# A two-layer decoder trunk: the first layer's down projection with tokens on partitions, turned back by transposes

## The chip, the cores and the metric

The kernel runs on one core of a Trainium2 chip. Times are device microseconds (us) of the whole execution. The kernel before took 593.86 us in the median of 3 runs (593.1 to 595.12).

## The reference

The input x has 256 tokens of 1024 features, in float32. Two layers follow each other. Layer 0 mixes tokens by DSA: an indexer scores all earlier tokens for each query, the 64 best are kept, and 8 heads attend over one shared latent. Layer 1 mixes by NSA: 8 heads attend over compressed blocks of keys and over two sets of keys and values (selected blocks and a window), and a gate weighs the three results. The keys and values of layer 1 are made once, from the stream behind layer 0. Each layer ends in the same MLP, and the output is normed. What the change touches is this:

```
def rmsnorm(x, g):
    y = x * rsqrt(mean(x * x, -1) + EPS)
    return y * g
x = x + relu(rmsnorm(x, g_mlp[l]) @ w_up[l]) ** 2 @ w_down[l]   # 1024 -> 4096 -> 1024
...
proj = rmsnorm(x, g_attn[0]) @ a_w_in[0]                        # head of layer 0
...
kv = rmsnorm(x, g_kv_shared) @ w_kv_shared                      # behind layer 0
```

## The kernel before, in words

Almost every operand of a product is split into a rounded part and a remainder, both in a format (fp32r) that TensorE takes in one pass. A product is then three matmuls (high by high, high by low, low by high), which `mm3` (line 96) issues. Weights come by DMA from SyncE's queue into 5 raw buffers; `weights` and `colw` (lines 135 to 149) let ScalarE round them (line 141) and VectorE form the remainder (line 142) into 8 weight buffers.

The stream is kept with features on partitions, as 8 tiles of 128 features by 256 tokens. The MLP (lines 776 to 819 for layer 0, from 1200 for layer 1) runs over 32 blocks of 128 hidden features. For block fi, `up` makes u (24 matmuls of 256 columns); ScalarE, GpSimd and VectorE square and split it; and the down projection of the block before adds to four PSUM banks. The last NDEF = 4 blocks are left for the end. In layer 0 the down projection is `KOuter` (line 597): the weight block is stationary, u's 256 tokens move, and the sum has features on partitions, so 24 matmuls of 256 columns per block. `finish` closes one bank after the other, each with an epilogue `end0` (line 812): VectorE adds the bank to the scaled stream x1 and gets x2 (512 columns); then for each of its two feature tiles ScalarE and VectorE form sh and sl (x2 times the gain, split) and ScalarE squares x2 for the norm; GpSimd adds the squares. In layer 1 the down projection has u stationary and 512 features of the weight block moving, so tokens are on partitions and a block takes 12 matmuls of 512 columns.

Behind layer 0 come the shared keys (line 830): kk, 96 matmuls that run over k = 0 to 7, the feature tiles of sh and sl, then kc (the tokens to be compressed, 4 times 24 matmuls by `projT`, in two banks), then the compressing products co, and the shared values v. The norm's factor is applied late: the mean of squares goes through a small matmul (after k = 4), VectorE and a power on GpSimd to r2; `bcast` (line 194, after k = 6) spreads r2 over all partitions by a matmul and a VectorE copy to Rb. Rb scales kk (line 863), kc (line 879) and the stream for layer 1 (xns on GpSimd, line 853).

At the head (lines 206 to 284) the input and a_w_in come in four pieces by SyncE's queue: the constants `vec` first, then xT and win of piece 0, 1, 2, 3. ScalarE's queue loads the bias table and its one-hot map. TensorE runs warm-up matmuls on ones, then the bias table's product `ups`, then the projection: 8 plain fp32 matmuls of 456 columns for piece 0 and 12 fp32r ones for each other piece. ScalarE squares xT (sqs), VectorE sums the squares and copies the projection out of its two banks (zc, line 314). One GpSimd power (line 355) gives three norm factors per token half, which the indexer's keys kd (line 362) and others wait for.

PSUM has 8 banks in two pools: psA (`acc=True`, 4 banks) and psB (4 banks). The framework orders instructions by its own estimate of time and adds all waits; `pin` keeps an instruction behind the one written before it on the same engine, and `behind(a, b)` issues a after b.

Of the kernel before, what the change touches and what calls it, by code (L numbers as in the profile page):

```python
# [50 lines left out]
def trunk(ctx: ExitStack, tc: tile.TileContext, I, out):  # L51
# [23 lines left out]
    def bigt(shape, dt, name):  # L75
        return big.tile(shape, dt, tag="big", name=name)
# [16 lines left out]
    def mm(ps, a, b, start, stop):  # L93
        return nc.tensor.matmul(ps, a, b, start=start, stop=stop, skip_group_check=True)  # L94

    def mm3(ps, ah, al, bh, bl, start, stop):
        mm(ps, ah, bh, start, False)
        mm(ps, ah, bl, False, False)
        mm(ps, al, bh, False, stop)

# [92 lines left out]

    def bcast(col2, name):

        ps = bank(name + "_ps")
        for i in range(2):
            mm(ps[:, i * P:(i + 1) * P], col2[:, i:i + 1].to_broadcast([P, P]), ident,
               i == 0, i == 1)
        b = kept([P, T], name)  # L200
        nc.vector.tensor_copy(b, ps[:, :T])
        return b


    new_phase("workA")
    vec = const.tile([P, NV], F32, name="vec")
    nc.sync.dma_start(vec, I["vecs"])
    mhalf = const.tile([P, 4], F32, name="mhalf")
# [15 lines left out]
    mm(ups[:H, :256], relb, oneh, True, True)  # L224
    for n in range(2):
        mm(wps[:, :P], ones, ones, True, True)
    usb = wk("pe", 4, [H, 384], "usb")
# [13 lines left out]

    xT = bigt([P, KT, T], F32, "xT")
    xgh = bigt([P, KT, T], F32R, "xgh")
# [6 lines left out]
    for j in range(4):  # L250
        pair = slice(2 * j, 2 * j + 2)
        nc.sync.dma_start(xT[:, pair], I["xT"][:, pair])
        raw = rawp.tile([P, 2, 456], F32, tag="raw", name=f"win{j}_raw")
        nc.sync.dma_start(raw.rearrange("p a m -> p (a m)"), I["a_w_in"][j])
        if j == 0:
            xg0 = k4([P, 2, T], "xg0")
            for k in range(2):
                nc.scalar.activation(xg0[:, k], xT[:, k], AF.Copy, scale=vec[:, V_GA + k:V_GA + k + 1])
        else:
            xh = nc.scalar.copy(xgh[:, pair], xT[:, pair])  # L260
            nc.vector.tensor_sub(xgl[:, pair], xT[:, pair], f(xgh[:, pair]))
            w = wp.tile([P, 2, 1024], F32R, tag="w", name=f"win{j}")
            wh, wl = (w[:, s, :912].rearrange("p (a m) -> p a m", a=2) for s in range(2))
            for a in range(2):
                g = vec[:, V_GA + 2 * j + a:V_GA + 2 * j + a + 1]
                hi_last = nc.scalar.activation(wh[:, a], raw[:, a], AF.Copy, scale=g)
                lo_last = nc.vector.scalar_tensor_tensor(wl[:, a], raw[:, a], g, f(wh[:, a]),
                                                         op0=OP.mult, op1=OP.subtract)
        for i in range(2):
            for a in range(2):  # L270
                k = 2 * j + a
                if j == 0:
                    mm(proj[i][:, :456], xg0[:, k, i * P:(i + 1) * P], raw[:, a], k == 0, False)
                    continue
                mm3(proj[i][:, :456], xgh[:, k, i * P:(i + 1) * P], xgl[:, k, i * P:(i + 1) * P],
                    wh[:, a], wl[:, a], False, k == KT - 1)
    for j in range(4):
        behind(nc.scalar.activation(sqs[:, j], xT[:, 2 * j:2 * j + 2], AF.Square), hi_last if j > 1 else xh)
    for j in range(1, 4):
# [74 lines left out]
    scs = const.tile([P, 2, 4], F32, name="scs")  # L354
    nc.gpsimd.tensor_tensor(scs[:, :, :3], ss[:, :, :3], mhalf[:, None, :3].to_broadcast([P, 2, 3]), op=OP.pow)
    pin(nc.gpsimd.tensor_tensor(scs[:, :, 3], msx, mhalf[:, :2], op=OP.pow))
# [420 lines left out]
    up = mlp_up(0, hh, hl, up_last)  # L777
    us, dws = {}, {}
    for fi in range(NF):
        us[fi] = up(fi)  # L780
        dws[fi] = colw(I["w_down"][0, fi], f"dn0_{fi}", after=up_last if fi < 2 else last if fi < 4 else None)
        if fi == 0:
            y = KOuter("y0")
        if 1 <= fi <= NF - NDEF:
            y.add(dws[fi - 1], us[fi - 1][:, 0], us[fi - 1][:, 1])
        if 4 <= fi < 4 + KT:
# [31 lines left out]

    y.finish([(dws[g], us[g][:, 0], us[g][:, 1]) for g in range(NF - NDEF, NF)], end0)


    new_phase("workN")
    def projT(ps, w, xh, xl, start):

        for k in range(KT):
            mm3(ps, w[0][:, k], w[1][:, k], xh[:, k], xl[:, k], start and k == 0, k == KT - 1)

# [5 lines left out]
    for k in range(KT):  # L833
        for g in range(G):
            for seg in range(2):
                wh, wl = kw[2 * g + seg]
                mm3(kk[g][:, seg * T:(seg + 1) * T], wh[:, k], wl[:, k], sh[:, k], sl[:, k],
                    k == 0 and seg == 0, k == KT - 1)
        if k == 4:
            ms2 = small([P, 2], "ms2")  # L840
# [4 lines left out]
            r2 = rsq(ms2, 2, "r2")  # L845
        if k == 6:
            Rb = bcast(r2, "Rb")

# [23 lines left out]
    for kv in range(2):  # L872
        ps = bank(f"kc{kv}")
        for g in range(G):
            projT(ps[:, g * T:(g + 1) * T], cw[2 * kv + g], sh, sl, g == 0)

# [510 lines left out]
```

## Time and profile before

| | |
|---|---|
| median of 3 runs | 593.86 us |
| the profiled execution | 593.29 us |
| its span (first to last instruction) | 591.5 us |
| TensorE busy with matmuls | 577.2 us, 98% |
| VectorE, ScalarE, GpSimd busy | 364.2, 320.4, 159.1 us |
| DMA | 103.97 MB, 176 GB/s mean |

The profiled execution lasted 1.79 us longer than its span. Matmuls overlap one another, so the duration of a single matmul is longer than the distance between the starts of two; the chain of waits, which follows the work that ended last, shows that distance in sums.

### The profile page before, as it was taken

How to read it: one execution, taken by the hardware profiler on the slowest of the kernel's cores; microseconds unless marked ns; L12 is line 12 of the kernel's file. 1: busy time of each engine (PE TensorE's matmuls, PEld its weight loads, DVE VectorE, ACT ScalarE, POOL GpSimd, SP SyncE). 2: the span in 40 equal slices, each digit the busy share in tenths (PEclk: the TensorE clock that was granted, in tenths of full speed). 3: DMA queues.
4: the chain of work that ended last, by engine and by line, in shares of the span. 5: the costliest groups of instructions: out<-in, count | busy, mean ns of one | idle time of the engine just before them, and what ended most of it. 6: DMA issues, size and time to landing. Idle time of an engine off the chain costs nothing.

```text
span 591.5 us, 10852 instructions
## 1 busy us (share of the span) xinstructions
PE 577.2 (98%) x4170; PEld 542.9 (92%) x4170; DVE 364.2 (62%) x612; ACT 320.4 (54%) x580; POOL 159.1 (27%) x225
## 2 busy tenths in 40 slices
PE   8899999999999999999999999999999999999995
PEld 6787899999999999999968999999899999999994
DVE  3897399544474444547897877639845444454523
ACT  6656666444444454436866878637544545454423
POOL 0155457010101011015530076808310110011012
PEclk9999999999999999999999999999999999999998
DMA  8911447765546656543499943314866665656201
GB/s 300 345 47 61 149 176 235 249 194 178 179 145 212 181 178 190 180 164 113 160 308 304 327 139 102 97 49 138 287 205 186 181 191 169 180 180 203 77 0 71
DMA packets 30475, 103.97 MB, mean 176 GB/s; under 512 B 3632, under 2 KB 5464, under 8 KB 30296
## 3 DMA queue, kind: packets, MB, share of 16 engines
q1 hardware_dynamic: 30024, 102.45, 53.7%
q10 hardware_dynamic: 400, 0.83, 0.5%
q8 instruction: 32, 0.52, 0.4%
q14 instruction: 19, 0.16, 0.1%
HBM read 102.21 MB, written 1.06 MB: 175 GB/s over the span
## 4 chain that ended last, share of the span: by engine, by line
PE 84%; DVE 9%; issue 2%; DMA 2%; ACT 1%; POOL 1%; SPq 1%; POOLq 0%; ACTq 0%; DVEq 0%
PE y L94 30%; PE u L94 28%; PE nq L94 4%; PE yb L94 3%; PE ya L94 3%; PE kk L94 2%; PE npo L94 2%; PE kc L94 1%; PE nl L94 1%; DVE c L903 1%; DMA win_raw<-in_a_w_in 1%; PE v L94 1%; PE co L94 1%; PE ix L94 1%; DMA wv_raw<-in_kvV 1%
## 5 line engine op out<-in xcount | busy, mean ns | idle before, releaser
L142 DVE TENSOR_TENSOR dn<-dn_raw,dn 128x1024 fp32r<-128x1024 f32 x64 | 80.6, 1260 | 99.2 <-ACT dn L141 99.2
L645 POOL TENSOR_TENSOR us<-ur 128x256 f32<-128x256 f32 x64 | 45.4, 711 | 282.0 <-ACT ur L642 282.0
L142 DVE TENSOR_TENSOR up<-up_raw,up 128x1024 fp32r<-128x1024 f32 x64 | 81.9, 1280 | 44.6 <-ACT up L141 44.6
L141 ACT CAST up<-up_raw 128x1024 fp32r<-128x1024 f32 x64 | 67.0, 1048 | 60.0 <-PE y L94 58.5
L94 PE MATMUL u<-h1h,up 128*128 128x256 f32 x512 | 97.0, 284 | 0.6 <-DVE up L142 0.6
L94 PE MATMUL y<-uu,dn 128*128 128x256 f32 x768 | 97.0, 283 | 0.3 <-DVE uu L647 0.3
L94 PE MATMUL u<-h0h,up 128*128 128x256 f32 x512 | 96.7, 283 | 0.0
L94 PEld LDWEIGHTS y<-uu,dn 128*128 128x128 f32 x768 | 94.2, 192 | 0.5 <-DVE uu L647 0.5
L94 PE MATMUL y<-dn,uu 128*128 128x512 f32 (+1 forms) x396 | 92.5, 384 | 0.0
L94 PEld LDWEIGHTS y<-dn,uu 128*128 128x128 f32 x396 | 71.1, 189 | 13.0
L94 PEld LDWEIGHTS u<-h1h,up 128*128 128x128 f32 x512 | 81.5, 191 | 1.6 <-DVE up L142 0.8
L642 ACT ACTIVATE ur<-u 128x256 f32<-128x256 f32 x64 | 24.6, 384 | 107.2 <-PE u L94 107.2
L94 PEld LDWEIGHTS u<-h0h,up 128*128 128x128 f32 x512 | 81.7, 192 | 0.0
L94 PE MATMUL u<-h1l,up 128*128 128x256 f32 x256 | 72.5, 283 | 0.0
L94 PE MATMUL u<-h0l,up 128*128 128x256 f32 x256 | 72.2, 283 | 0.0
L141 ACT CAST dn<-dn_raw 128x1024 fp32r<-128x1024 f32 x64 | 66.7, 1042 | 7.2 <-PE y L94 3.0
L94 PEld LDWEIGHTS u<-h1l,up 128*128 128x128 f32 x256 | 49.0, 191 | 0.9
L94 PEld LDWEIGHTS u<-h0l,up 128*128 128x128 f32 x256 | 49.1, 192 | 0.0
L647 DVE TENSOR_TENSOR uu<-us,uu 128x256 fp32r<-128x256 f32 x64 | 29.1, 455 | 8.1 <-POOL us L645 8.1
L646 ACT ACTIVATE uu<-ur 128x256 fp32r<-128x256 f32 x64 | 26.7, 417 | 0.1
L94 PE MATMUL ya<-oT,wo 128*128 128x256 f32 x192 | 25.2, 288 | 0.3 <-DVE oT L591 0.3
L94 PE MATMUL nq<-ah,wq 128*128 128x256 f32 x128 | 24.9, 286 | 0.0
(300 smaller groups left out, 966.8 us busy)
## 6 DMA issues: line engine op xcount, KB each, us to landing
up_raw<-in_w_up SPq DMA_DIRECT2D x64, 512.0 KB, 3.7
dn_raw<-in_w_down SPq DMA_DIRECT2D x64, 512.0 KB, 3.7
c1raw<-in_cmp_w SPq DMA_DIRECT2D x16, 512.0 KB, 4.9
wo_raw<-in_a_w_o SPq DMA_DIRECT2D x8, 512.0 KB, 4.1
wq_raw<-in_b_w_q SPq DMA_DIRECT2D x8, 512.0 KB, 5.9
wn_raw<-in_b_w_o SPq DMA_DIRECT2D x8, 512.0 KB, 4.9
wk_raw<-in_kvT SPq DMA_DIRECT2D x4, 512.0 KB, 3.6
wc_raw<-in_kvT SPq DMA_DIRECT2D x4, 512.0 KB, 3.6
```

The costliest lines, as they stand in the source:

```text
L94: return nc.tensor.matmul(ps, a, b, start=start, stop=stop, skip_group_check=True)
L141: ins = [hi(w[:, 0, :C], raw[:, :C]) if hi else nc.scalar.copy(w[:, 0, :C], raw[:, :C]), (lo or nc.vector).tensor_sub(w[:, 1, :C], raw[:, ...
L142: (lo or nc.vector).tensor_sub(w[:, 1, :C], raw[:, :C], f(w[:, 0, :C]))]
L642: nc.scalar.activation(r, ps[:, :T], AF.Relu)
L645: nc.gpsimd.tensor_tensor(s, r, r, op=OP.mult)
L646: nc.scalar.activation(u[:, 0], r, AF.Square)
L647: nc.vector.tensor_sub(u[:, 1], s, f(u[:, 0]))
L903: lo = nc.vector.tensor_sub(w4[:, :, 1], r4, f(w4[:, :, 0]))
```

## The change

It has four parts. The down projection of layer 0 takes layer 1's form (u stationary, 512 features moving, tokens on partitions). Its four banks yt[i][c] (token half i, feature half c) are closed in a written order, copied to SBUF by ScalarE (the last one half by VectorE), and 16 transposes by TensorE bring them back to features on partitions, from where `end0` goes on as before. The norm's small matmul moves behind k = 7, and `bcast` behind the first 24 matmuls of kc, whose banks now come from psA. At the head xT of piece 0 is issued first on SyncE's queue, and win of piece 0 and `vec` on ScalarE's; one warm-up matmul is added behind `ups` and three are pinned there; the squares of pieces 0 and 1 go behind the last split of the weights. The power of line 355 is cut in two: the keys' factor first.

```diff
-    def bcast(col2, name):
+    def bcast(col2, name, after):
...
-            mm(ps[:, i * P:(i + 1) * P], col2[:, i:i + 1].to_broadcast([P, P]), ident,
-               i == 0, i == 1)
+            behind(mm(ps[:, i * P:(i + 1) * P], col2[:, i:i + 1].to_broadcast([P, P]), ident, i == 0, i == 1), after)
...
+    xT = bigt([P, KT, T], F32, "xT")
+    pin(nc.sync.dma_start(xT[:, 0:2], I["xT"][:, 0:2]))
+    raw0 = rawp.tile([P, 2, 456], F32, tag="raw", name="win0_raw")
+    pin(nc.scalar.dma_start(raw0.rearrange("p a m -> p (a m)"), I["a_w_in"][0]))
     vec = const.tile([P, NV], F32, name="vec")
-    nc.sync.dma_start(vec, I["vecs"])
+    pin(nc.scalar.dma_start(vec, I["vecs"]))
...
-    for n in range(2):
-        mm(wps[:, :P], ones, ones, True, True)
+    for n in range(3):
+        pin(mm(wps[:, :P], ones, ones, True, True))
...
-        behind(nc.scalar.activation(sqs[:, j], xT[:, 2 * j:2 * j + 2], AF.Square), hi_last if j > 1 else xh)
+        behind(nc.scalar.activation(sqs[:, j], xT[:, 2 * j:2 * j + 2], AF.Square), hi_last)
...
-    nc.gpsimd.tensor_tensor(scs[:, :, :3], ss[:, :, :3], mhalf[:, None, :3].to_broadcast([P, 2, 3]), op=OP.pow)
+    pin(nc.gpsimd.tensor_tensor(scs[:, :, 2], ss[:, :, 2], mhalf[:, :2], op=OP.pow))
+    pin(nc.gpsimd.tensor_tensor(scs[:, :, :2], ss[:, :, :2], mhalf[:, None, :2].to_broadcast([P, 2, 2]), op=OP.pow))
...
+    def down(g, i, c, first, last, pinned=False):
+        mm3(yt[i][c], us[g][:, 0, i * P:(i + 1) * P], us[g][:, 1, i * P:(i + 1) * P],
+            dws[g][0][:, c * 512:(c + 1) * 512], dws[g][1][:, c * 512:(c + 1) * 512], first, last, pinned)
...
         if 1 <= fi <= NF - NDEF:
-            y.add(dws[fi - 1], us[fi - 1][:, 0], us[fi - 1][:, 1])
+            for i in range(2):
+                for c in range(2):
+                    down(fi - 1, i, c, fi == 1, False)
...
-    y.finish([(dws[g], us[g][:, 0], us[g][:, 1]) for g in range(NF - NDEF, NF)], end0)
+    ysb = bigt([P, 2, 2, 512], F32, "ysb")
+    turned = {}
+
+    def finish0(i, c):
+        for g in range(NF - 2, NF):
+            down(g, i, c, False, g == NF - 1, True)
+        if (i, c) == (1, 1):
+            nc.scalar.copy(ysb[:, i, c, :256], yt[i][c][:, :256])
+            nc.vector.tensor_copy(ysb[:, i, c, 256:], yt[i][c][:, 256:])
+        else:
+            nc.scalar.copy(ysb[:, i, c], yt[i][c])
+
+    def turn0(i, c):
+        for b in (2 * c, 2 * c + 1):
+            if b not in turned:
+                turned[b] = bank(f"yT{b}", acc=b > 1)
+            for a in range(2):
+                pin(nc.tensor.transpose(turned[b][:, a * T + i * P:a * T + (i + 1) * P],
+                                        ysb[:, i, c, (2 * (b % 2) + a) * P:(2 * (b % 2) + a + 1) * P], ident))
+            if i == 1:
+                end0(b, turned[b])
+
+    for g in range(NF - NDEF, NF - 2):
+        for i in range(2):
+            for c in range(2):
+                down(g, i, c, False, False)
+    finish0(0, 0)
+    finish0(1, 0)
+    finish0(0, 1)
+    turn0(0, 0)
+    turn0(1, 0)
+    finish0(1, 1)
+    turn0(0, 1)
+    turn0(1, 1)
...
-        if k == 4:
+        if k == 7:
             ms2 = small([P, 2], "ms2")
...
-        if k == 6:
-            Rb = bcast(r2, "Rb")
+
+    kc = [bank(f"kc{kv}", acc=True) for kv in range(2)]
+    Rb = bcast(r2, "Rb", projT(kc[0][:, :T], cw[0], sh, sl, True))
```

## Rows read from the trace of the kernel before

**Rows 1.** The page's first line, its part 1 (busy time of each engine, share of the span, instructions) and from part 2 the granted TensorE clock in 40 slices (9 is 90% of full speed or more).

```profile
span 591.5 us, 10852 instructions
PE 577.2 (98%) x4170; PEld 542.9 (92%) x4170; DVE 364.2 (62%) x612; ACT 320.4 (54%) x580; POOL 159.1 (27%) x225
...
PEclk9999999999999999999999999999999999999998
```

**Rows 2.** The chain of work that ended last, in order of time (start us, length us, what), in and behind the first layer's MLP.

```profile
116.22 2.88 PE u L94 x24
119.10 2.88 PE y L94 x24
...
258.21 11.52 PE y L94 x96
269.73 7.20 PE kk L94 x60
...
282.13 8.65 PE kc L94 x72
```

**Rows 3.** The same chain in the second layer's MLP, whose down projection has tokens on partitions already.

```profile
455.61 2.87 PE u L94 x24
...
487.04 2.75 PE y L94 x12
...
492.66 2.75 PE y L94 x12
...
498.71 2.76 PE y L94 x12
...
573.22 8.20 PE y L94 x36
```

**Rows 4.** The tile x3t, whose four banks are filled by four 128x128 transposes each in the second layer's MLP: one view of its instructions (count, then ns min/median/max, first and last start).

```profile
L1231 PE MATMUL x3t<-cst,x x16: 270/272/273, 495.2 to 513.7; 128*128 128x128 f32 x16
L1232 ACT COPY x3t<-x3t x4: 580/582/584, 496.4 to 514.6; 128x512 f32<-128x512 f32 x4
```

**Rows 5.** Timeline of all engines around the first projection's end (start us, us, engine, line, operation, out<-in, count, idle before and who ended it): VectorE's and ScalarE's reads of the same two banks.

```profile
17.11 0.37 PE L94 MATMUL proj<-win,xgl 128*128 128x456 f32 x1
17.41 0.75 DVE L314 COPY zc<-proj 128x256 f32<-128x256 f32 x2
...
17.86 0.28 ACT L351 ACTIVATE junk<-proj 128x128 f32<-128x128 f32 x1 [2.10 <-DVE zc L314]
```

**Rows 6.** Timeline of VectorE alone behind the first layer's MLP (same columns).

```profile
264.73 0.69 DVE L813 TENSOR_TENSOR x<-y,x 128x512 f32<-128x512 f32 x1 [3.51 <-PE y L94]
266.00 0.48 DVE L160 SCALAR_TENSOR_TENSOR sl<-x,vec,sh 128x256 fp32r<-128x256 f32 x1 [0.58 <-ACT sh L159]
...
273.61 5.04 DVE L142 TENSOR_TENSOR wc<-wc_raw,wc 128x1024 fp32r<-128x1024 f32 x4 [0.87 <-ACT wc L141]
...
281.73 1.23 DVE L903 TENSOR_TENSOR c<-c1raw,c 128x1024 fp32r<-128x1024 f32 x1 [3.02 <-ACT c L902]
282.87 0.42 DVE L201 COPY Rb<-Rb_ps 128x256 f32<-128x256 f32 x1
...
292.44 5.71 DVE L903 TENSOR_TENSOR c<-c1raw,c 128x1024 fp32r<-128x1024 f32 x4
298.08 1.05 DVE L879 TENSOR_TENSOR x<-kc,Rb 128x512 f32<-128x512 f32 x1
```

**Rows 7.** VectorE's busy time in one stretch (stretch us, its length, busy us and instructions, granted clock, DMA share, GB/s), and from the timeline of all engines the start of the shared values' projection.

```profile
281.70:325.00 43.30, 39.29 (x46) 1.00 0.77 256
...
299.77 0.42 PEld L94 LDWEIGHTS v<-wv,sh 128*128 128x128 f32 x2
```

**Rows 8.** Timeline of all engines at the kernel's head (same columns as rows 5; SPq and ACTq are the queues that issue DMAs).

```profile
0.73 0.39 SPq L207 DMA_DIRECT2D vec<-in_vecs  x1
...
1.02 4.14 PE L94 MATMUL warm_ps<-ones 128*128 128x128 f32 x20 [1.02 <-POOL ones L211]
1.18 0.42 SPq L252 DMA_DIRECT2D xT<-in_xT  x1
...
1.25 0.36 ACTq L220 DMA_DIRECT2D oneh<-in_onehot  x1
...
4.95 0.91 ACT L258 ACTIVATE xg<-xT,vec 128x256 f32<-128x256 f32 x2 [2.27 <-DMA xT<-in_xT]
...
5.09 0.59 PE L94 MATMUL ups<-oneh,relb 32*8 32x256 f32 x2
...
6.34 3.30 PE L94 MATMUL proj<-win_raw,xg 128*128 128x456 f32 x8 [0.66 <-DMA win_raw<-in_a_w_in]
```

**Rows 9.** The same timeline from the fourth piece of the input weights to the indexer's keys.

```profile
12.25 1.15 ACT L278 ACTIVATE sqs<-xT 128x512 f32<-128x512 f32 x2
...
15.22 2.28 DVE L280 TENSOR_TENSOR sqs<-sqs 128x512 f32<-128x512 f32 x3
...
20.22 1.35 POOL L355 TENSOR_TENSOR scs<-ss,mhalf 128x6 f32<-128x6 f32 x1 [1.92 <-DVE ss L353]
...
21.54 0.70 POOL L356 TENSOR_TENSOR scs<-msx,mhalf 128x2 f32<-128x2 f32 x1
...
22.10 0.50 PE L364 MATMUL tk<-cst,kd 128*128 128x128 f32 x2 [0.71 <-DVE kd L362]
...
24.16 2.00 PE L94 MATMUL ix<-kiT,qiT 128*128 128x128 f32 x16
```

More of the change, by code (lines that the diff above doesn't have):

```diff
@@ L94, in mm, with mm3 @@
         return nc.tensor.matmul(ps, a, b, start=start, stop=stop, skip_group_check=True)
-    def mm3(ps, ah, al, bh, bl, start, stop):
-        mm(ps, ah, bh, start, False)
+    def mm3(ps, ah, al, bh, bl, start, stop, pinned=False):
+        ins = mm(ps, ah, bh, start, False)
+        if pinned:
+            pin(ins)
         mm(ps, ah, bl, False, False)
-        mm(ps, al, bh, False, stop)
+        return mm(ps, al, bh, False, stop)
     def behind(ins, prev):
@@ L238, in bias_keys @@
         return biasT[:, h, :ns][:, ::-1]
-    xT = bigt([P, KT, T], F32, "xT")
     xgh = bigt([P, KT, T], F32R, "xgh")
@@ L251, in trunk @@
         pair = slice(2 * j, 2 * j + 2)
-        nc.sync.dma_start(xT[:, pair], I["xT"][:, pair])
-        raw = rawp.tile([P, 2, 456], F32, tag="raw", name=f"win{j}_raw")
-        nc.sync.dma_start(raw.rearrange("p a m -> p (a m)"), I["a_w_in"][j])
+        raw = rawp.tile([P, 2, 456], F32, tag="raw", name=f"win{j}_raw") if j else raw0
+        if j:
+            nc.sync.dma_start(xT[:, pair], I["xT"][:, pair])
+            nc.sync.dma_start(raw.rearrange("p a m -> p (a m)"), I["a_w_in"][j])
         if j == 0:
@@ L778, in trunk @@
     us, dws = {}, {}
+    def down(g, i, c, first, last, pinned=False):
+        mm3(yt[i][c], us[g][:, 0, i * P:(i + 1) * P], us[g][:, 1, i * P:(i + 1) * P],
+            dws[g][0][:, c * 512:(c + 1) * 512], dws[g][1][:, c * 512:(c + 1) * 512], first, last, pinned)
     for fi in range(NF):
         us[fi] = up(fi)
-        dws[fi] = colw(I["w_down"][0, fi], f"dn0_{fi}", after=up_last if fi < 2 else last if fi < 4 else None)
+        dws[fi] = weights(I["w_down"][0, fi], f"dn0_{fi}", after=up_last if fi < 2 else last if fi < 4 else None)
         if fi == 0:
-            y = KOuter("y0")
+            yt = [[bank(f"y0{i}{c}", acc=True) for c in range(2)] for i in range(2)]
         if 1 <= fi <= NF - NDEF:
-            y.add(dws[fi - 1], us[fi - 1][:, 0], us[fi - 1][:, 1])
+            for i in range(2):
+                for c in range(2):
+                    down(fi - 1, i, c, fi == 1, False)
         if 4 <= fi < 4 + KT:
@@ L825, in projT @@
         for k in range(KT):
-            mm3(ps, w[0][:, k], w[1][:, k], xh[:, k], xl[:, k], start and k == 0, k == KT - 1)
+            ins = mm3(ps, w[0][:, k], w[1][:, k], xh[:, k], xl[:, k], start and k == 0, k == KT - 1)
+        return ins
     kk = [bank(f"kk{g}") for g in range(G)]
@@ L872, in trunk @@
     for kv in range(2):
-        ps = bank(f"kc{kv}")
+        ps = kc[kv]
         for g in range(G):
-            projT(ps[:, g * T:(g + 1) * T], cw[2 * kv + g], sh, sl, g == 0)
+            if kv or g:
+                projT(ps[:, g * T:(g + 1) * T], cw[2 * kv + g], sh, sl, g == 0)
         ff = x1f[:, 544 * kv:544 * (kv + 1)].rearrange("p (b c) -> p b c", c=34)
```

## Prediction

> **What bounds the kernel now.** I read the page's shares first: TensorE has matmuls in 98% of the span, VectorE and ScalarE are near 60% and 54%, and the granted clock is full in all slices but the last [rows 1]. So a change pays only where it takes work or waits off TensorE, or off whatever TensorE waits for. The chain of waits in order of time then tells the stages apart. In layer 0's MLP the chain alternates 24 matmuls of u and 24 of y, 2.88 us each, without a gap (2.88 / 24 = 0.120 us a matmul); the last four blocks' 96 matmuls take 11.52 us, and kk starts at their end, 269.73 [rows 2]. TensorE alone bounds this stage. Layer 1, which has the new form already, takes 2.75 us for a block's 12 matmuls of 512 columns (0.229 us each) beside the same u, and 8.20 us for 36 of them at its end (0.228) [rows 3]. From kc on it is different: from 281.7 to 325 us VectorE is busy for 39.29 of 43.3 us [rows 7], and TensorE waits for its casts. At the head, TensorE and VectorE wait in turn for transfers, squares and a GpSimd power [rows 8, 9].
>
> **Down projection.** Each of 28 blocks in the loop goes from 2.88 to 2.75 us: 28 x 0.13 = 3.6 us less. The last four go from 11.52 to 48 x 0.229 = 11.0: 0.5 less. Together -4.2 us [rows 2, 3]. The weights are cast as before, so the other engines' work in the loop doesn't change, and layer 1 shows that they keep up with a block of 5.62 us (487.04 to 492.66) [rows 3].
>
> **The way back.** Added are 16 transposes, three ScalarE copies of 512 columns, and one bank copied in two halves. In layer 1, where four transposes of the same size stand between two blocks, a block takes 6.05 us (492.66 to 498.71) instead of 5.62: 0.43 us for four, 0.11 each [rows 3]. One by itself lasts 0.27 us [rows 4]. The bounds are 16 x 0.11 = 1.7 and 16 x 0.27 = 4.3 us; they are issued back to back like those four, so I take +1.7.
>
> The copies: a ScalarE copy of a bank lasts 0.58 us [rows 4]. The first three have a further six matmuls (1.37 us) or eight transposes ahead of their reader, and are hidden. The last bank, (1,1), has only the four transposes of (0,1), 0.43 us, before TensorE wants it. Its halves: ScalarE about 0.35 (from 0.58 for a whole bank), VectorE 0.42 as the equally large Rb copy [rows 6]. They share a bank, and where ScalarE read a bank that VectorE was reading, it waited for VectorE though it needs nothing of its result (junk, released by zc) [rows 5]; so they go one after the other, about 0.9 with the hand-over. 0.9 - 0.4 = +0.5 us. Bounds: 0, if kk's first products fill the gap, and 1.2, if an addition of end0 (0.69 [rows 6]) is ahead in VectorE's queue.
>
> What comes late next is end0. It starts some 2.9 us before the last transpose (six matmuls, eight transposes, the wait). VectorE's part is 4 x 0.69 + 8 x 0.48 + 0.42 = 7.0 us [rows 6], so it ends about 4.1 us after kk's start. kk runs k from 0 and takes 1.44 us per k (12 x 0.120); the banks of k = 4 to 7 are wanted 5.8 us after its start. Hidden, with 1.7 us to spare for k = 4. The casts of wc behind it (5.04 us) come about 1 us later against kk; VectorE then idled 3.02 us [rows 6]. Nothing lost.
>
> **Norm and broadcast.** With kk's start later against its squares, the norm's matmul goes behind k = 7: the same four small instructions at another place, 0 us on TensorE. Its power on GpSimd (0.70 for two columns [rows 9]) lies beside the 24 matmuls of kc, 24 x 0.120 = 2.88 us, ahead of the broadcast. Against kk's end, Rb comes about 2.5 us later. Queued behind it on VectorE are kk's scaling, the keys' split and kc's emptying, on GpSimd the whole xns line. But VectorE has casts of c that need only kk's weight buffers: three of 1.23 us [rows 6], 3.7 us, before the fourth, which is held behind the first split fr. VectorE bounds this stage by its sum [rows 7], and the sum stays. Bounds -0.5 and +2.5 (the whole delay exposed); I take 0, since the casts cover it.
>
> **Head.** xT of piece 0 is issued 0.45 us sooner (1.18 to 0.73) and win of piece 0 about 0.9 sooner than as third on SyncE's queue; all later issues of SyncE move up by two places [rows 8]. The bytes stay. But `vec` now stands behind win's 456 KB in ScalarE's queue, and xg needs it; the bias table and its map, which `ups` needs, come behind both, some 0.9 us later. xg's first half takes 0.46 us, and the first product came at 6.34, when win landed [rows 8]; now it comes at win's landing plus 0.46, between 5.9 and 6.8. `ups` ran at 5.09 right behind the warm-ups. If it waits for its map until 6, three warm-ups of 0.41 us (4.14 us for ten, two instructions each) are pinned behind it, and the first product comes at 7.3 [rows 8]. So -0.4 to +0.9 at the projection's start. At its end, 17.48 [rows 5], I take 0: the later pieces come no later, and waits between them shrink when the start slips.
>
> The squares of pieces 0 and 1 (1.15 us) leave ScalarE's path ahead of the last split, so VectorE's sum (15.22 to 17.50), which stands behind that split, starts earlier; its last square comes as before. Then the first zc no longer waits for the sum but for its bank, and only the second is left behind the projection: -0.3 us (half of 0.75) [rows 5, 9]. The keys' power goes from 1.35 us for six columns to 0.70 as for two: -0.65, and TensorE waited 0.71 us there for kd, so it is on the path [rows 9]. The other two powers end about 0.35 us later than before against the first; they are wanted by the scores, after 2 us of key products [rows 9]. Head: -0.9 us, bounds -1.9 and +0.3.
>
> **Sum.** -4.2 + 1.7 + 0.5 + 0 - 0.9 = -2.9 us. Against the profiled execution (span 591.5, 593.29 with what lies around it) that is 590.4; that execution stands 0.57 us below the median of the runs, so against the median, which I use, 593.86 - 2.9 = 591.0.
>
> **The rivals.** *Everything falls well:* the last copy's gap is filled and the head gives its best: -4.2 + 1.7 - 1.9 = -4.4, 589.5. For it: the gaps are short. Against: `vec` behind win.
> *The head gives nothing:* `ups` and its warm-ups hold the first product: +0.3 in place of -0.9, so -1.7 and 592.2. For it: the one-hot map's place in the queue [rows 8]. Against: the power's 0.65 is independent of it.
> *Rb becomes the wait:* the order is fixed by the framework's estimate; if VectorE's queue has Rb's users ahead of the casts, it idles the 2.5 us: -0.4, 593.5, no change. For it: the stage is VectorE's. Against: casts are ready.
> *The slower side, a bank:* kc's two banks now belong to the four that co and v use, so v's second bank can be written only when kc's second is emptied. That ended at 299.13 behind four casts of 5.71 us; v started at 299.77 [rows 6, 7], and its second bank is wanted six matmuls (1.37) later, a slack of 2.0 us, from which on it decides. If the emptying comes 2.5 us later with Rb and behind four more casts, TensorE stands 2.5 + 5.7 - 2.0 = 6.2 us: +3.3, 597.2. Against: nothing in the change adds casts there.
> *The clock:* if the granted clock fell to the lower level in the turning, kk's 96 matmuls would cost up to 11.5 us more (twice 96 x 0.120): about 602. Against it: the clock is full in every slice with transposes [rows 1]. The Trainium skill, TensorE: Matmul & The Clock Gate, section Part 4: PE-mode transpose, says that transposes don't count as TensorE activity in the same way and don't bring the full clock; by that the sixteen, half of them in one run with a wait, are where it could fall. The rows speak against it at four transposes in a run; eight in a run no row shows.
>
> **How the numbers follow.** Forecast 0.58, its own range 589.9 to 592.1; falls well 0.10; head gives nothing 0.11; Rb 0.13; bank 0.06; clock 0.02. A measurement of this kernel tells about 0.3%, 1.8 us, from no change, so faster means below 592.1: nearly all of the forecast (0.55), falls well (0.10) and half of the head's case (0.05), 0.70. Slower: bank and clock, 0.08. The rest, 0.22, is the same. The range reaches from 589.0 to 594.0: it leaves out the two slow cases and the edges.
>
> **What would show it.** Right: y rows of 512 columns at 0.229 us, x384 in layer 0; 16 transposes in about 1.7 us; a TensorE gap of half a microsecond before the last four; kk starting about 2.9 us earlier on the span's scale; the first power 0.70 us and TensorE's wait for kd nearly gone. Wrong: a wait of kk for sl; VectorE idle for 2 us before Rb; v waiting for kc's emptying; the first product after 7 us; a clock below full at the turn.

## The result and the profile after: 1% slower

The changed kernel takes 599.0 us (median of four runs, 597.58 to 599.79) against 593.89 (four runs): a ratio of 1.0084, interval 1.0061 to 1.0108. The forecast was 591.0, range 589.0 to 594.0. The profiled execution took 598.93 us, its span is 597.2, 5.7 us longer.

The page after, first line, part 1 and the granted clock, against [rows 1]:

```profile
span 597.2 us, 10120 instructions
PE 578.4 (97%) x3804; PEld 525.8 (88%) x3804; DVE 367.4 (62%) x613; ACT 321.7 (54%) x584; POOL 159.1 (27%) x226
PEclk9999999999999999999999999999999999999998
```

TensorE's sum tells little here: it is 1.2 us longer, with 366 matmuls fewer. The loop has 4.1 us less of it, but 2.8 us more are counted up to the end of the first projection, for one warm-up more, and 2.3 more in the two stretches behind the loop: a busy TensorE is not one at full pace. The chain of waits of the changed kernel, in order of time (start us, length us, what), answers to [rows 2]:

```profile
109.16 2.87 PE u L94 x24
112.03 2.75 PE y L94 x12
...
250.56 8.63 PE u L94 x72
259.19 9.55 PE y L94 x42
268.74 0.87 PE yT L852 x8
269.61 1.38 PE y L94 x6
271.43 4.31 PE kk L94 x36
```

The loop does what it should: 2.75 us a block for 2.88, the last four blocks 9.55 + 1.38 us for 11.52, and eight transposes in 0.87 us, 0.11 each. To see where the time went I set four marks, read from each run's timeline: the start of the MLP's first product u, the end of its last u, the end of the last key product kk, and the end of the last product of the compression, co. Behind the last mark the two kernels take the same time (261.87 against 261.71 us to layer 1's last down product).

| | first u | u's last end | last kk | last co |
|---|---|---|---|---|
| before | 83.81 | 258.21 | 281.69 | 322.56 |
| after | 89.18 | 259.18 | 283.60 | 328.17 |
| change of the stretch | +5.37 | -4.40 | +0.94 | +3.70 |

The loop and the turn together give 3.46 us, more than forecast. The head loses 5.37, and between the last key product and the last compression product 3.70 more go, a stretch in which the change alters almost nothing. The views of these two places come with the experiments.

### The profile page after: what moved, and what is told of

It is laid out like the page before. It is cut to its first block, busy times and chain, and to the rows that moved or that the text cites. A ratio compares the mean times of both kernels' runs of the same rounds, so it can differ in the third digit from the quotient of the medians.

```text
span 597.2 us, 10120 instructions
## 1 busy us (share of the span) xinstructions
PE 578.4 (97%) x3804; PEld 525.8 (88%) x3804; DVE 367.4 (62%) x613; ACT 321.7 (54%) x584; POOL 159.1 (27%) x226
## 3 DMA queue, kind: packets, MB, share of 16 engines
HBM read 102.21 MB, written 1.06 MB: 173 GB/s over the span
## 4 chain that ended last, share of the span: by engine, by line
PE 83%; DVE 8%; DMA 3%; issue 3%; ACT 2%; POOL 0%; POOLq 0%; ACTq 0%; SPq 0%; DVEq 0%
PE u L94 30%; PE y L94 29%; PE ya L94 4%; PE nq L94 4%; PE yb L94 3%; PE proj L94 2%; PE npo L94 2%; PE nl L94 1%; DVE c L955 1%; DMA c1raw<-in_cmp_w 1%; DMA xT<-in_xT 1%; DVE score L473 1%; DVE score L484 1%; PE po L94 1%; DMA wv_raw<-in_kvV 1%
## 5 line engine op out<-in xcount | busy, mean ns | idle before, releaser
L94 PE MATMUL y<-dn,uu 128*128 128x512 f32 (+1 forms) x780 | 185.5, 388 | 0.0
L94 PEld LDWEIGHTS y<-dn,uu 128*128 128x128 f32 x780 | 141.2, 189 | 26.3
L94 PE MATMUL yb<-nTh,wn 128*128 128x256 f32 x128 | 24.8, 284 | 0.1
L94 PEld LDWEIGHTS ya<-oT,wo 128*128 128x128 f32 x192 | 23.8, 191 | 1.1 <-DVE oT L599 0.5
```

## Experiments

Medians and ratios are against runs of the kernel before on the same chip (its medians there 593.35 to 593.85). The last column of marks is the stretch from the first u to the last co, which leaves the head out.

| run | first u | last kk | Rb copied | last co | co less u | median us | ratio, interval |
|---|---|---|---|---|---|---|---|
| before | 83.81 | 281.69 | 282.87 | 322.56 | 238.75 | 593.86 | |
| after | 89.18 | 283.60 | 290.81 | 328.17 | 238.99 | 599.0 | 1.0084 (1.0061 to 1.0108) |
| e1 old head | 84.94 | 279.34 | 286.23 | 324.16 | 239.22 | 595.42 | 1.0036 (1.0023 to 1.0049) |
| e2 new head alone | 87.09 | 284.96 | 286.14 | 326.16 | 239.07 | 596.83 | 1.0058 (1.0037 to 1.0080) |
| e3 vector first | 88.51 | 282.91 | 289.70 | 326.94 | 238.43 | 597.36 | 1.0065 (1.0050 to 1.0080) |
| e4 and in turn | 86.63 | 281.04 | 287.89 | 324.99 | 238.36 | 597.86 | 1.0080 (1.0063 to 1.0096) |
| e5 kk held | 88.95 | 285.76 | 291.00 | 327.85 | 238.90 | 598.82 | 1.0077 (1.0052 to 1.0102) |
| e6 kk held, copies first | 88.24 | 283.44 | 289.40 | 328.40 | 240.16 | 597.94 | 1.0062 (1.0037 to 1.0086) |
| e7 Rb alone | 83.85 | 281.28 | 286.52 | 322.94 | 239.09 | 594.48 | 1.0012 (0.9997 to 1.0028) |
| e8 power alone | 83.76 | 281.63 | 282.81 | 322.35 | 238.59 | 592.89 | 0.9978 (0.9964 to 0.9992) |
| e9 filled head | 85.42 | 279.81 | 286.58 | 324.13 | 238.71 | 594.7 | 1.0020 (1.0008 to 1.0033) |
| e10 old head, old Rb | 85.58 | 279.99 | 285.09 | 323.83 | 238.25 | 595.93 | 1.0033 (1.0014 to 1.0052) |
| e11 old head, early casts | 85.68 | 282.13 | 287.38 | 324.79 | 239.11 | 595.75 | 1.0031 (1.0018 to 1.0045) |
| e12 e10 and e11 | 85.73 | 280.74 | 285.09 | 325.53 | 239.80 | 596.11 | 1.0034 (1.0016 to 1.0052) |
| e13 Rb mid | 85.74 | 280.60 | 283.29 | 322.99 | 237.25 | 593.65 | 1.0007 (0.9994 to 1.0020) |
| e14 early casts, kc held | 85.51 | 280.53 | 285.77 | 322.53 | 237.02 | 592.97 | 0.9991 (0.9978 to 1.0003) |
| e15 e13 and e14 | 85.78 | 281.23 | 284.47 | 323.09 | 237.31 | 593.72 | 1.0004 (0.9989 to 1.0019) |
| e16 three casts | 85.69 | 282.69 | 285.09 | 323.43 | 237.74 | 594.12 | 1.0024 (1.0007 to 1.0041) |
| e17 e14 with a bridge | 85.09 | 280.09 | 285.33 | 321.71 | 236.62 | 592.7 | 0.9979 (0.9966 to 0.9991) |
| e18 e6, old head | 87.54 | 282.80 | 288.76 | 326.58 | 239.04 | 594.79 | 1.0003 (0.9985 to 1.0021) |

### The head: e1 to e4, e9

The timeline of the changed kernel's head (columns as [rows 8], which it answers to):

```profile
0.73 0.40 SPq L209 DMA_DIRECT2D xT<-in_xT  x1
1.19 1.41 SPq L259 DMA_DIRECT2D xT<-in_xT  x3
6.33 1.37 SPq L260 DMA_DIRECT2D win_raw<-in_a_w_in  x3
0.73 0.40 ACTq L211 DMA_DIRECT2D win_raw<-in_a_w_in  x1
1.16 0.45 ACTq L213 DMA_DIRECT2D vec<-in_vecs  x1
6.72 0.15 DVE L431 TENSOR_SCALAR gkvs<-vec 128x1 f32<-128x1 f32 x1 [6.72 <-DMA vec<-in_vecs]
7.38 0.62 ACT L266 CAST xgh<-xT 128x512 fp32r<-128x512 f32 x1 [4.25 <-DMA xT<-in_xT]
7.91 0.90 ACT L264 ACTIVATE xg<-xT,vec 128x256 f32<-128x256 f32 x2
1.02 3.78 PE L94 MATMUL warm_ps<-ones 128*128 128x128 f32 x16 [1.02 <-POOL ones L217]
8.46 5.90 PE L94 MATMUL proj<-win_raw,xg 128*128 128x456 f32 x8 [3.66 <-ACT xg L264]
14.30 0.59 PE L94 MATMUL ups<-oneh,relb 32*8 32x256 f32 x2
14.82 0.94 PE L94 MATMUL warm_ps<-ones 128*128 128x128 f32 x6
```

Four things went otherwise than I had worked out. `vec`, behind win, was there only at 6.72 (2.74 before, by the same instruction of VectorE); and the framework put the split of piece 1 ahead of xg, so ScalarE waited for that piece's transfer and xg came at 7.91 instead of 4.95. It put `ups` and the three pinned warm-ups behind the first eight products, so TensorE stood idle from 4.80 to 8.46. The eight products then took 5.90 us instead of 3.30. And SyncE issued the inputs of pieces 1 to 3 at once and their weights only at 6.33, after 3.7 us that the view of waits puts down to the landing of piece 0's weights; before, they went out between 2.6 and 5.2 us. The trace says why: the program counts landings on a few semaphores in turn, and the ninth DMA of the head takes the first one's again and is not issued before that one has landed. Here the first was piece 0's weights on ScalarE's queue, landed at 6.32; before, it was the bias table of 1 KB, landed at 2.55.

**e1** takes the head back:

```diff
-    pin(nc.scalar.dma_start(raw0.rearrange("p a m -> p (a m)"), I["a_w_in"][0]))
-    pin(nc.scalar.dma_start(vec, I["vecs"]))
+    nc.sync.dma_start(vec, I["vecs"])
...
```

> The changed kernel with the head put back as it was: the weight of the last norm's gains, the inputs and the first projection's four pieces all issued by SP in turn, two free warm-up products, the early squares where they were. The split power, the down projection in 512 columns, the turning back and the later broadcast stay. Head theory (the gains' vector lands 4 us later behind the first piece on ScalarE's queue, SP holds the other three pieces back, and the projection then runs at half pace): the MLP's first product comes back from 89.2 to about 83.5 us, and since nothing between there and the end gives slack, the whole run falls by about 5.4 us against the changed kernel: 593.5 us, a tie with the kernel before. Rival (the head's delay is mostly regained later, and the 5 us are lost in the turn and the projections behind it): the first product comes early, but the run falls by less than 2 us, 597 us or more.

First u at 84.94, 4.24 us earlier, and 3.6 us off the median. So the head costs 3 to 4 us, and it isn't regained; but 2.1 us over the kernel before remain, which falls between the theories: 1.1 us of it still lie ahead of the first u, and what the loop gains is lost behind the last key product.

**e2** is the kernel before with this head alone.

> The kernel before with the new head alone (first piece and gains on ScalarE's queue, three pinned warm-ups, squares behind the casts). Head theory: about 5 us slower than before, 599 us, first MLP product at 89 us. Rival (head alone is harmless, the loss needs the rest): within 1 us of before.

First u 3.28 us later, median 3.5 us up. Harmful by itself, if less than the 5 us expected.

**e3** issues `vec` first on ScalarE's queue; **e4** also pins SyncE's inputs and weights in turn:

```diff
+            pin(nc.sync.dma_start(xT[:, pair], I["xT"][:, pair]))
+            pin(nc.sync.dma_start(raw.rearrange("p a m -> p (a m)"), I["a_w_in"][j]))
```

> The changed kernel, with the gains' vector issued ahead of the first piece of the weight on ScalarE's queue; nothing else. If the vector behind the 456 KB piece is what costs: first scaled operand at about 5.4 us instead of 7.9, first product near 6, TensorE not idle for 3.7 us, and some 3 to 5 us are regained (594 to 596 us). If instead SP's late pieces 1 to 3 (issued at 6.3 us) set the projection's end: the first product is earlier but the projection ends within 1 us of 23.2, and the run gains less than 1.5 us (597.5 us or more).

> As the run with the vector first, and SP's inputs and pieces are held in turn (input 1, piece 1, input 2, piece 2, ...) as in the kernel before, so that piece 1 is issued near 2 us. If the late pieces are what costs, the projection's end comes back to about 17 to 18 us and the run to about 593.5 us. If the half pace of the first products is a matter of the clock and not of the data, the projection still ends behind 20 us and the run stays above 595.5 us.

In e3 xg starts at 5.29, but TensorE then waits for the first piece until 7.99: first u only 0.67 us earlier. In e4 it is 2.55 us earlier by the profile, but that was the fastest of its four runs, and the median doesn't show it (597.86, from 595.8 to 598.6). With `vec` first on ScalarE's queue the ninth DMA waits for `vec`: it went out at 5.28 in e3 and at 4.33 in e4, each 0.02 us behind the landing. In both the eight products stay slow (5.76 and 4.79 us); in e4:

```profile
7.08 4.79 PE L94 MATMUL proj<-win_raw,xg 128*128 128x456 f32 x8 [2.27 <-DMA win_raw<-in_a_w_in]
```

**e9** goes on from e4 with 13 warm-ups ahead of the first product and none behind.

> The run with the vector first and inputs and pieces in turn, and now 13 free warm-up products ahead of the first product instead of 8, and none pinned behind the first eight products. If the half pace of the first eight products (0.6 to 0.76 us each instead of 0.41) comes of TensorE standing idle for 2.3 us ahead of them: they take 3.3 us again, and with the three warm-ups gone from the middle the projection ends near 18.5 us instead of 20.7; run 2 us below that one (595.5 to 596 us). If they go at half pace because of their own data, they still take 4.8 us and the projection ends behind 20 us.

The same products in e9:

```profile
7.96 3.30 PE L94 MATMUL proj<-win_raw,xg 128*128 128x456 f32 x8 [1.26 <-DMA win_raw<-in_a_w_in]
```

The eight products take 3.30 us again, the projection ends at 19.44 instead of 20.72, and the median falls by 3.2 us to 594.7, more than the 1.2 us by which the profiles' first u moves. So the data didn't make them slow. That the shorter wait ahead of them (1.26 us for 2.27) brought the pace back fits, but isn't shown: other runs have the low pace behind shorter waits (last section).

### The turn: e5, e6, e18

The changed kernel's turn, from its timelines of TensorE, ScalarE and VectorE:

```profile
275.57 0.38 PE L852 MATMUL yT<-cst,ysb 128*128 128x128 f32 x2
276.26 0.38 PE L852 MATMUL yT<-cst,ysb 128*128 128x128 f32 x2
272.69 0.35 ACT L842 COPY ysb<-y 128x256 f32<-128x256 f32 x1
273.58 0.41 DVE L843 COPY ysb<-y 128x256 f32<-128x256 f32 x1
275.99 1.39 DVE L828 TENSOR_TENSOR x<-yT,x 128x512 f32<-128x512 f32 x2 [1.99 <-PE yT L852]
280.72 3.75 DVE L144 TENSOR_TENSOR wc<-wc_raw,wc 128x1024 fp32r<-128x1024 f32 x3 [0.20 <-ACT wc L143]
290.81 0.42 DVE L202 COPY Rb<-Rb_ps 128x256 f32<-128x256 f32 x1
```

The last bank was finished at 270.99, but its two copies ended at 273.04 and 273.99: the work of the first two residual blocks is ahead of them on both engines. 36 key products went ahead of the last transposes. So VectorE got the last blocks at 275.99, and the casts of wc started at 280.72, 2.9 us before the last key product; before the change it was 8.1 us before it (273.61 and 281.69).

**e5** pins the key products behind the transposes, **e6** also orders the second residual block behind the copies:

```diff
-                    k == 0 and seg == 0, k == KT - 1)
+                    k == 0 and seg == 0, k == KT - 1, k == 0)
...
+        if b:
+            behind(add, copies[1])
```

> The changed kernel, with the first products of the key projection (k = 0, four groups) held in program order behind the last eight transposes, so that none of its 36 products can slip ahead of the last bank's way back. If the slip is what delays the residual and the cast of the next weights: the last two blocks of x2 come about 2 us earlier, the casts of the compressed keys' weights too (279.65 to about 277.5 us), and the run gains 1.5 to 3 us (596 to 597.5 us). If the slip only fills TensorE while it would wait in any case: TensorE is idle for 3 to 4 us at 271 us instead, the products move behind it, and the run is within 1 us of the changed kernel or slower by up to 3 us.

> As the run before, and the last bank's two copies go ahead of the second residual block (its addition and its scaled operands are ordered behind the copies). Turn theory (the copies stand 1.7 to 2.7 us behind the work for the first two blocks on ScalarE and VectorE, and this decides when the last blocks and the next weights' casts come): copies end near 272 us instead of 274, last casts 3 us earlier, run 3 to 5 us below the changed kernel (594 to 596 us). Rival (the end of the turn is hidden under the key projection; what costs is somewhere else): within 1 us of the changed kernel.

In e5 the last transposes come 2.4 us earlier, the key products end 2.2 us later, and the last co ends where it did: the slip had only filled TensorE. e6 was blurred, as TensorE's clock was low for part of the values (granted clock 0.57 from 316 to 320 us, behind a wait of 2.32 us for wv). Its median lies 1.06 us below the changed kernel, between the two theories. So **e18** repeats it with the old head.

> The repaired turn (key products behind the last transposes, last bank's copies ahead of the second residual block) once more, now with the old head, since the first run of it lost some 1.7 us to a stretch at the lower clock in the shared values. Turn theory: the copies and casts come 2 to 3 us earlier than in the run with the old head alone, and the run comes to 592.5 to 593.5 us. VectorE theory: the casts of the compressed keys' weights come only about 1 us earlier, Rb none, and the run stays within 1 us of 595.4 us.

First u to last co takes 239.04 us for e1's 239.22, and the median is 0.6 us below e1's, which speaks for the VectorE theory: by the marks the order of the turn has next to no share. The times are less sure: e18's runs spread from 592.3 to 597.0, the profiled one is the slowest, and against the kernel before its interval (0.9985 to 1.0021) lies below e1's (1.0023 to 1.0049), so that a gain of up to 2 us isn't excluded.

### The stretch behind the last key product: e7, e8, e10 to e17

Busy time of each engine in two stretches, from the last u to the last kk and from there to the last co (stretch, length, busy us of TensorE, weight loads, VectorE, ScalarE, GpSimd, clock, DMA share, GB/s), before and then after:

```profile
258.21:281.69 23.48, 23.48 (x199) 23.48 (x198) 14.04 (x21) 12.57 (x25) 8.04 (x11) 1.00 0.40 127
281.69:322.56 40.87, 39.49 (x222) 33.63 (x222) 38.09 (x44) 29.61 (x40) 12.62 (x11) 1.00 0.77 255
```

```profile
259.18:283.60 24.42, 24.42 (x164) 22.22 (x162) 13.09 (x20) 13.49 (x28) 6.74 (x10) 1.00 0.22 57
283.60:328.17 44.57, 40.81 (x227) 34.02 (x226) 39.70 (x45) 29.31 (x40) 11.88 (x12) 1.00 0.76 267
```

The second stretch grows by 3.70 us: VectorE has 1.61 us more to do in it (39.70 for 38.09), casts of wc among it that used to lie ahead, and stands idle 2.09 us longer (4.87 for 2.78). Two explanations were open, Rb's lateness and VectorE's queue on the one hand, the loads of the compression's weights on the other (57 GB/s in the first stretch for 127, since their buffers are held by wc until its casts).

**e7** and **e8** are the kernel before with the later broadcast alone and the split power alone.

> The kernel before with only the later mean and broadcast (after the last key product, the broadcast behind the first compressed-key projection, whose banks come from the accumulators). If the later Rb is hidden as forecast: within 0.6 us of before. If it is exposed, as in the third rival: 2 to 3.5 us slower (596 to 597.5 us).

> The kernel before with only the split power (keys first). Forecast 0.65 us faster, because the index keys wait for the power alone. If the path to the first index scores goes by another wait, within 0.3 us.

e7: Rb is copied 3.65 us later and the last co ends 0.38 us later, a tie: as forecast, hidden, while TensorE comes to this stretch as late as before. e8: 0.96 us faster, about the forecast's 0.65; in its profile the keys' transposes start 0.58 us sooner, but the first u moves by only 0.05 and the last co by 0.21, so where the median's gain arises isn't shown.

**e10**: e1 and the old mean and broadcast. **e11**: e1, and two casts of wc ordered behind the second residual block instead of the last:

```diff
-f"wc{j}", after=tail)
+f"wc{j}", after=tails[1] if j < 2 else tail)
```

**e12**: both.

> The changed kernel with both the head and the mean and broadcast put back as before; left of the change are the split power, the down projection in 512 columns and the turning back. The key and compressed-key products of the run with the old head end 1.9 us ahead of the kernel before, but the compression and the values end 1.6 us behind it. Theory Rb (the later broadcast, Rb 3.4 us later than before, sets VectorE's and ScalarE's work for that stage, now that TensorE gets there earlier): Rb comes near 281 us, the stage ends near 321 us, and the run is 2 to 3 us below the one with the old head: 592.5 to 593.5 us. Theory loads (the stage is held by the compression's weights, whose loads wait for the buffers of the compressed keys' weights, cast at 275.4 us instead of 272.5): no gain, 595 us.

> The changed kernel with the old head, and two of the four casts of the compressed keys' weights go ahead of the last two residual blocks, into the 3.4 us that ScalarE stands idle there. Theory loads: two buffers come free some 5 us earlier, the compression's weights land earlier, and the run is 1.5 to 2.5 us below the one with the old head (593 to 594 us). Theory Rb: within 0.7 us of it.

> Both of the last two edits together (old head, old mean and broadcast, two early casts). If Rb and the loads each hold the stage, only this run gets the loop's 4 us: 590 to 592 us, below the kernel before. If one of them alone holds it, this run equals the better of the two before it.

All three are within 0.7 us of e1, each for a reason of its own. In e10 (timeline and stretches of TensorE) the old broadcast stands in TensorE's own queue:

```profile
282.68 0.71 PE L94 MATMUL Rb_ps<-cst,r 128*128 128x128 f32 x4 [2.35 <-POOL r L193]
...
280.00:284.00 4.00, 1.66 (x13) 0.94 0.86 279
284.00:288.00 4.00, 4.00 (x25) 0.64 0.95 366
```

The squares now end late against the key products, so TensorE waits 2.35 us for the power, and goes at a clock of 0.64 for the 4 us behind. Even so e10's stretch from first u to last co is 1.0 us shorter than e1's; in its profile 2 us go again behind the last co (263.9 us to layer 1's last down product for 261.9). So whether moving the broadcast was needed with this loop isn't shown. In e11, 19 products of kc slipped ahead of the last of kk, which ended 2.0 us later behind the first u than in e1, and Rb with it; e12 has e10's wait (2.74 us). So neither theory was tested cleanly. e1's VectorE shows what else holds Rb: its matmul started at 283.58, but its copy stands behind two remainders whose casts on ScalarE wait for their loads.

```profile
283.31 1.23 DVE L950 TENSOR_TENSOR c<-c1raw,c 128x1024 fp32r<-128x1024 f32 x1 [0.78 <-ACT c L949]
285.09 1.23 DVE L950 TENSOR_TENSOR c<-c1raw,c 128x1024 fp32r<-128x1024 f32 x1 [0.55 <-ACT c L949]
286.23 0.42 DVE L202 COPY Rb<-Rb_ps 128x256 f32<-128x256 f32 x1
```

**e13** to **e16** repair that: in e13 the mean stands between k = 6 and 7 of the key products, the broadcast behind the fifth step of the first kc projection, and Rb's copy ahead of the second cast; e14 is e11 with kc's first product held behind the last kk; e15 is both, e16 e15 with three early casts.

```diff
-        if k == 7:
+        if k == 6:
             ms2 = small([P, 2], "ms2")
...
+        elif kv == 0 and c:
+            behind(lo, copied[0])
```

> The changed kernel with the old head; the mean of squares stands between the last two steps of the key products, the broadcast behind the fifth step of the first compressed-key projection, and Rb's copy ahead of the second and later compression casts on VectorE. VectorE theory: Rb comes near 282.5 us instead of 286.2, VectorE loses some 2 us less to waiting, and the compression ends near 322 us instead of 324.2: run 1 to 2 us below the one with the old head (593.5 to 594.5 us). Theory loads: Rb is early, the stage's end stays within 0.7 us.

> The changed kernel with the old head; two of the four casts go ahead of the last residual blocks, and the compressed-key products are held behind the key products (in the run with the early casts 24 of them had slipped ahead, and the key products ended 2.8 us later). VectorE theory: two casts (2.3 us) leave the stretch, but Rb stays late, so about half comes back: 593.5 to 594.5 us. Theory loads: buffers come free 5 us earlier, all of it comes back: 592 to 593 us.

> Both: early Rb, two early casts, key products in order. VectorE theory: the stretch behind the last key product takes 40 to 41 us again as before the change, the compression ends near 320 us, and the run comes to 590.5 to 592.5 us, 1 to 3 us below the kernel before. If something else holds the stage (loads, or the products themselves), it stays above 593.5 us.

> As the run before with three early casts. VectorE theory: the third cast, 1.1 us, goes ahead of the last residual blocks, whose additions it delays by about as much; within 0.7 us of the run with two.

Rb in e13, from its timeline:

```profile
282.48 0.60 PE L94 MATMUL Rb_ps<-cst,r 128*128 128x128 f32 x4
283.29 0.41 DVE L207 COPY Rb<-Rb_ps 128x256 f32<-128x256 f32 x1
```

e13 and e14 each take 2 us out of the stretch from first u to last co and 1.8 and 2.4 us off e1's median. In e13 no load is earlier (58 GB/s ahead of the last kk, as in e1), so the late Rb is shown as a cause by itself. e14's 592.97 lies in the range of the loads theory, not in that of VectorE's; but its casts both free buffers (98 GB/s ahead of the last kk) and leave VectorE's stretch, so it doesn't part the two. The view of waits, of the second stretch before and after, says that the loads have a share (us in total, times, longest):

```profile
ACT c L902 <- DMA c1raw<-in_cmp_w: 2.2, 5, 0.8
```

```profile
ACT c L954 <- DMA c1raw<-in_cmp_w: 7.8, 9, 2.1
```

It is 6.3 us in e1, 2.7 in e13 and 3.6 in e14. e16 has more bytes loaded ahead of the last kk than the kernel before (123 GB/s x 26.98 us = 3.3 MB for 127 x 23.48 = 3.0) and gains nothing on e14, so earlier loads bring nothing more there; how the 3.70 us divide between Rb and the loads stays open. The gains don't add: e15 misses its 590.5 to 592.5. The second stretch of e14 and of e16 tells why:

```profile
280.53:322.53 42.00, 40.01 (x227) 34.11 (x226) 37.48 (x43) 28.87 (x40) 12.98 (x12) 1.00 0.76 260
```

```profile
282.69:323.43 40.74, 39.23 (x223) 33.74 (x222) 37.68 (x44) 29.04 (x40) 13.35 (x11) 1.00 0.74 253
```

The stretch is back to before's length in e16, but the last kk comes 2.6 us later behind the first u than in e1 (197.0 for 194.4), where the casts taken out of the stretch now stand ahead of the last blocks' additions. And in e14 TensorE is counted busy for 40.0 of the 42.0 us. Of the loop's 4.4 us, 1.7 reach the last co in e14 (237.02 against 238.75).

**e17** adds four warm-ups to e14:

```diff
-    for n in range(2):
+    for n in range(6):
         mm(wps[:, :P], ones, ones, True, True)
```

> The run with the two early casts and the key products in order, and now 14 free warm-up products instead of 10 ahead of the first projection, as a bridge to its operand, which in every kernel with the new loop lands about 1 us later than before. Theory of the idle TensorE: the first eight products take 3.3 us again instead of some 4.3, everything behind moves up by about 1 us, and the run comes to 591.5 to 592.5 us, some 0.2 to 0.3 per cent below the kernel before. If the pace is not set by the idle time, it equals the run with 10 warm-ups (593 us) or is up to 0.5 us slower, as the one-hot product stands behind the longer bridge.

The heads of e14 and then e17:

```profile
5.58 1.02 PE L94 MATMUL ups<-oneh,relb 32*8 32x256 f32 x2
7.34 4.81 PE L94 MATMUL proj<-win_raw,xg 128*128 128x456 f32 x8 [0.75 <-DMA win_raw<-in_a_w_in]
```

```profile
6.64 0.59 PE L94 MATMUL ups<-oneh,relb 32*8 32x256 f32 x2
7.30 3.30 PE L94 MATMUL proj<-win_raw,xg 128*128 128x456 f32 x8
```

With no gap ahead of them the eight products are at full pace. But the first product comes no sooner than in e14, the first u only 0.42 us sooner, and the median of 592.7 us lies 0.3 below e14's and just above the range that was expected. With a ratio of 0.9979 (0.9966 to 0.9991) this version beats the kernel before by 0.2%, and the changed one by 6 us. The split power alone (e8) reaches the same, 0.9978, and is part of e17: that the new loop brings anything on top of it is not shown by the times.

## Why the prediction was wrong, point by point

- **Down projection, -4.2, and the way back, +1.7 + 0.5.** Right, or a little better: by the marks -4.40 for the loop's -3.6, and +0.94 for the last four blocks and the turn (-0.5 + 1.7 + 0.5 = +1.7); -3.46 together for -2.0. The transposes take 0.11 us each. The half microsecond of the last bank's copies was wrong in both directions: they ended 3.0 us behind the bank, past the bound of 1.2, but TensorE didn't stand, as key products filled the gap (the bound of 0).
- **Head, -0.9, bounds -1.9 and +0.3.** The step that failed is "At its end, 17.48, I take 0: the later pieces come no later". The projection ended at 23.19. I worked from the program's order and took the framework's order on each queue for the same; what it put ahead of xg and of `ups` was decided anew, and the weights of the later pieces waited for the landing of piece 0's on the other queue. The lower bound, -1.9, doesn't come out of the terms: -0.4 - 0.3 - 0.65 is -1.35. The rival "the head gives nothing" named `ups` and its warm-ups, but with them ahead of the first product; behind it they did the opposite, and left TensorE idle. The Trainium skill, DMA: Bandwidth & Descriptors, section Issuing engines are not separate DMA queues, says that issuing on several engines saves only the sequencer's time to issue; this head agrees, as two queues bought 0.45 us of issue for piece 0's input, and the first product came 2.1 us later (0.95 in e2, with the old loop).
- **"The casts of wc behind it come about 1 us later against kk ... Nothing lost."** They came 5.2 us later against it (they start 2.9 us ahead of its end for 8.1). I had end0 end 4.1 us behind kk's start, at 275.5 here; its last split ends at 280.52.
- **Rb, "I take 0, since the casts cover it".** Against kk's end it was copied 6.0 us later (7.21 behind it for 1.18), not 2.5: its matmul started 4.2 us behind kk's end, where it had started 0.2 ahead of it, and its copy then waited in VectorE's queue behind remainders whose casts waited for loads. e7 shows that 3.65 us are covered as long as TensorE comes late; with the loop's gain they aren't, and an earlier Rb gives 2 us back (e13). The wrong sentence is "VectorE bounds this stage by its sum, and the sum stays": in the stretch from kk's end VectorE had 1.61 us more to do and idled 2.09 longer. And if its sum bounds (39.29 of 43.3 us [rows 7]), a TensorE that arrives 3 us earlier must wait for it. The rival of the exposed Rb came nearest, with 2.5 us where the stretch lost 3.7, but by another way: it had Rb's users ahead of the casts, and in the runs the casts stood ahead of Rb.
- **The rivals of the bank and of the clock at the turn** didn't happen: v wasn't held by kc's emptying, and the clock was full through eight transposes in a run. A lower clock came elsewhere (e6, e10, e12). The power of two columns took 0.73 us for the forecast's 0.70.

Left open: with the old head, every kernel with the new loop gets its first operand about 1 us later than those with the old loop (e1's first product at 7.54 for 6.34), though the first DMAs are issued in the same order at the same times; the first transfers are slower (piece 0's input landed at 6.18 for 4.86), and no run tells why. The chip isn't it: with the old head the chip of e1 (new loop) is late against that of e7 and e8 (old loop, 6.39 and 6.62), with the new head the chip of e7 and e8 (e5, new loop, 8.32) against that of e1 (e2, old loop, 7.29). This is part of the 2.1 us that e1 lost. Open too is how the loss behind the last key product divides between Rb and the loads.

## What to carry to other kernels

A gain on the engine that bounds one stage can be lost to the engine that bounds the next (of the loop's 4.4 us, 1.7 came through in e14): read the next stage's busy sums before counting it, and look for what the change pushes into that engine's queue. A transfer moved to another queue, or a pinned filler, changes what an ordering framework puts around it; what TensorE does until its first operand lands is part of that edit's price. A large transfer issued first can hold back later ones of another queue that count on its semaphore. An order that hid a step in the old kernel must be tried again with the new one: a later Rb cost nothing with the old loop (e7), an earlier one gave 2 us with the new (e13).

## What the runs showed of the hardware

- TensorE's pace behind a gap at the head. Eight products of 456 columns took 3.30 us (before, e1, e8, e9, e16, e17; 3.33 in e7) or 4.77 to 6.19 (all others). TensorE was idle ahead of them for 0.75 us in e14, at the lower pace, and for 1.54 in e16, at the full: the gap alone doesn't decide. With none (e17) the pace was full. The view of stretches says 1.00 for 8 to 12 us in the changed kernel, though its products go at half pace (its record of the clock begins at 13.7 us); in e13 and e6 it gives 0.57 and 0.61 for the same 4 us: at the head this column is not to be relied on.
- GpSimd's power of two columns for Rb takes 0.71 us or 1.62, nothing between. In all 20 profiles it is 1.62 (13 times) where VectorE had begun a remainder of 1024 columns, of two SBUF operands, 0.15 to 0.17 us before it, and 0.71 (7 times, before among them) where VectorE stood idle at its start, even if a remainder began before its end (e6, e15, e18). The Trainium skill, Trainium Architecture — The Big Picture, section What this means for kernel authors, says that these two engines share a port pair under an exclusive lock; the two values agree, though no run here was made for it.
- TensorE's granted clock behind a wait in mid-kernel. It fell below full in a stretch of 4 us shortly behind waits of 2.32 us (e6, 0.57), 2.35 us (e10, 0.64) and 2.74 us (e12, 0.60), and was full again in the next stretch.
